# Turning the attention weights of an encoder layer by VectorE blocks and a trip through DRAM instead of by TensorE

## The chip, the cores and the metric

The kernel runs on one core of one Trainium2 chip. The core has five engines with instruction streams of their own: TensorE (PE: matmuls; its weight loads are listed as PEld), VectorE (DVE), ScalarE (ACT), GpSimd (POOL) and SyncE (SP). Each works through its stream in order and waits on semaphores. SP here does nothing but issue DMAs, POOL mostly issues DMAs; the transfers run on 16 DMA engines that all queues share. The metric is the device time of one execution in microseconds.

## What is computed

One encoder layer over 1024 positions of width 1024, in float32: a SwiGLU block, a mixer, and a second SwiGLU block, each followed by a layer norm. The change lies in the mixer's attention:

```python
HEAD_DIM = 128
ATTN_PATTERNS = ((128, 1), (512, 4), (2048, 16))     # (window, dilation), 4 heads each
# Query i attends to i + dilation*j for |j| <= window/(2*dilation), i.e. 64 keys to each side
s = einsum(q, k) * scale + bias(masked)
p = exp(s - max(s))
den = sum(p)
o = einsum(p, v) / den
# the three groups' outputs are then mixed by softmax over their log-sum-exps
attn = sum(softmax(lse over groups) * o)
```

With the scores computed as queries (partitions) by keys (columns), the exponentials p have to be turned to keys by queries before they can be multiplied with v.

## The kernel before

Large products are computed by a Strassen-like scheme: a block of output channels is seven products (`PROD`, jobs `J[c, 1]` to `J[c, 7]`), each job twelve matmuls of 128x128 by 512 columns (each operand split in a high and a low part, three terms). The mixer's projection runs over pairs of channel blocks: two for the Fourier branch, then twelve that give the queries and keys of one head each, then eight for the gates. The twelve heads go in four slots `h`, in each of them group `g` 0, 1, 2 (dilation 1, 4, 16). The attention of a head is done while the projections of later pairs run: its small matmuls are put between the jobs.

A head's attention goes in steps (`one(si, step)`); a step holds two query tiles (four in group 2):

| group | steps per head | query tiles x keys of a step |
|---|---|---|
| 0 | 4 | three of 2 x 256, one of 2 x 192 (the first and last tile) |
| 1 | 4 | 2 x 192 |
| 2 | 2 | 4 x 128 |

That makes 40 steps. A step of width 192 is called split in the code (`split_`). Each step is a chain over the engines:

1. `scores`: TensorE, into a PSUM bank `sc`.
2. `add_bias`: VectorE, from PSUM to a half page `p` in SBUF (scale and bias; the 256-wide form keeps 192 of the keys of each tile, packed as 384 columns).
3. `top`: VectorE, row maxima. `exps`: ScalarE, exponentials in place, with row sums.
4. `turn`: TensorE, transposes of 128x128 blocks (`cuts`: three for the widths 256 and 192, two for group 2) into a PSUM bank `pt`.
5. `blank`: VectorE, zeros into the parts of the turned tile `pT` that are masked (not for split steps). `turned`: ScalarE, the copy of `pt` into `pT`.
6. `values`: TensorE, three or four matmuls with the values `v` (and `ve`, the values at the windows' edges), into a PSUM bank `pv`.
7. `keep`: ScalarE, the copy into the head's output page `pv`, which POOL stores to DRAM (`pv_d`). A later part (`combine`) loads these pages again (`pw`) and mixes the groups.

The values are loaded by `load_values` (SP, from `v_spill`, in rows of 512 bytes, two to seven DMAs a head), the bias by `load_bias` (POOL), the weights of the next projections by `pair_load` (SP: `gq`, `uq`, 512 KB each).

The order on every engine is fixed when the program is built, by a planner written into the kernel (`Flow`). It has one node for each piece of work, with a booked cost, the nodes it depends on, and the buffers that it takes and gives back: 8 PSUM banks (`b`), 46 pages of 4 KB per partition (`p`) and 14 half pages (`h`). `fl.job` nodes make up TensorE's main sequence, in a given order. `V`, `S` and `G` nodes are work of VectorE, ScalarE and POOL, taken by urgency when the planner's clock of that engine comes to them. `F` nodes are floating TensorE work, such as the steps' matmuls: at each job boundary those are put in whose inputs were ready 0.8 us before. `Q` nodes are loads issued on SP: at each job boundary those are issued whose time has come and whose inputs exist. They are booked on one clock of the DMA engines:

```python
    RATE, LAND, STORE, KEEP = 0.36, 2.5, 3.5, 4
...
            self.dma = max(self.dma, t) + n.cost / self.RATE
            self.finish(n, self.dma + self.LAND)
```

The cost is in MB, the rate in MB per us. POOL's stores are booked on the same clock. In a dependency written `(node, w)` the planner adds `w` us behind the node. The booked figures decide the order only; on the chip every instruction waits for its real inputs, in the order of its engine. A DMA that reads what another has written waits on SP until that one has landed.

Of the kernel before, what the change touches and what calls it, by code (L numbers as in the profile page):

```python
# [16 lines left out]
P = 128  # L17
# [26 lines left out]
PAIRS = 11  # L44
FIRST = 3
MIDK = 36
LEADS = [0, 1, 2, 3, (0, 1), (1, 1), (2, 1), (3, 0), (4, 0), (5, 0), (3, 1), (4, 1), (5, 1)]


# [29 lines left out]
class Flow:  # L79
# [207 lines left out]
class Builder:  # L287
# [10 lines left out]
    def half(self, name, dt=F32):  # L298
        return self.sb.tile([P, 512], dt, name=name, tag="s2", bufs=NS2)
# [4 lines left out]
    def bank(self, name):  # L304
        return self.pp.tile([P, 512], F32, name=name, tag="ps", bufs=8)
# [6 lines left out]
def kernel(  # L312
# [40 lines left out]
    W, B, H, J = {}, {}, {}, {}  # L353
# [998 lines left out]
    for i, (to, x0, x1) in enumerate((("t1", "b11", "b12"), ("t3", "b12", "b22"), ("t2", "t1", "b22"),  # L1352
# [16 lines left out]
    for i, (to, x0, x1) in enumerate((("t1", "b11", "b12"), ("t3", "b12", "b22"), ("t2", "t1", "b22"),  # L1369
# [11 lines left out]
        n = Q(J[("a", 5 + i), 4], 0.6, copy, [ttn[x0]] if x0 in ttn else [], lead=0.0)  # L1381
# [109 lines left out]
    qt = V(0.4, third_row, [q2], VJ["t", 6, 0], halves=1)  # L1491
# [255 lines left out]
    last_turn = [None, None]  # L1747

    def attention(idx, g, h, qk, qk_nodes):
        c = PC["q", idx]  # L1750
        env = {}
        qv = Q(J[c, 4], 0.5, lambda: env.__setitem__("v", load_values(g, h)),
               [(n, 4.0) for m in range(8) for n in (v_stored[g, m] if g == 2 else [v_stored[g, m]])], 12.0, pages=1 + int(g == 0),
               halves=int(g == 1))
        qb = Q(J[c, 4], 0.1, lambda: env.__setitem__("b", load_bias(g, h)),
               [(shear_n[g * SLOTS + h], 4.0)] + ([bias_done[idx - 2]] if idx >= 2 else []), 12.0)
# [10 lines left out]
        if g == 0:  # L1767
            qk_nodes = [split(f"{'qk'[i]}s{h}", lambda i=i: qk[i], lambda t, i=i: qk_parts.__setitem__(i, t), qk_nodes[i])
                        for i in range(2)]
        else:  # L1770
            qk_nodes = qk_nodes[0] + qk_nodes[1]
        exp_n.setdefault(h, [])

        def one(si, step):
            n, w = len(step), step[0][2]
            pw = 64 if w == P else 192
            st = {}
# [34 lines left out]
            tiles = sorted(qt for qt, _, _ in step)  # L1812
# [12 lines left out]
                                         accum_out=stats[h][:, k, 1:2])  # L1825
            (qa, ka, _), (qb_, kb_, _) = step[0], step[1]
            cuts = [0, P] if w == P else [0, 2 * P, P]
            where = [(qa, ka), (qb_, kb_ + 64)] if w == 192 else [(qa, qa * P), (qb_, qb_ * P)] if w == 256 else []

            def turn():  # L1830
                st["tp"] = ps = bank(f"pt{g}{h}{si}")
                flat = st.pop("p")
                for sl, x in enumerate(cuts):
                    nc.tensor.transpose(ps[:, sl * P:(sl + 1) * P], flat[:, x:x + P], ident)

            split_ = w == 192
# [5 lines left out]
                nc.vector.memset(t[64:P, :, 0:64], 0.0)  # L1842

            def turned():
                if split_:
                    st["t"] = half(f"pT{g}{h}{si}")
                t, tp = st["t"], st["tp"]
                k = 0
                if w > P:
                    k = 2 * P  # L1850
                    nc.scalar.activation(t[:, :k], tp[:, :k], AF.Copy)
                if split_:
                    to, at = (x[:, k:k + P].rearrange("p (s q) -> p s q", s=2) for x in (t, tp))
                    nc.scalar.activation(to, at[:, ::-1, :], AF.Copy)
                    return
                to = t[:, k:].rearrange("p (n q) -> p n q", q=P)
                at = tp[:, k:k + (512 - k) // 2].rearrange("p (n q) -> p n q", q=64)
                for ps_ in (slice(0, 64), slice(64, P)):
                    nc.scalar.activation(to[ps_, :, ps_], at[ps_], AF.Copy)

            def values():
                st["o"] = bk = bank(f"pv{g}{h}{si}")
                by_half = bk.rearrange("p (r a) -> p r a", a=64)
                pt = st.pop("t")

                def add(out, v, sl, start, stop):
                    nc.tensor.matmul(out, v, pt[:, sl * P:(sl + 1) * P], start=start, stop=stop, skip_group_check=True)  # L1867
                if w == P:
                    for i in range(4):
                        r = 4 * (i // 2) + i % 2  # L1870
                        add(by_half[:, r:r + 3:2, :], env["v"][tiles[0] + i], i, True, True)
                    return
                for i, (qt, k0) in enumerate(where):
                    at = tiles.index(qt) * P
                    add(bk[:, at:at + P], env["v"][k0, P], i, i == 0, False)
                if split_:
                    add(bk[:, 64:192], env["v"]["edge", ka], 2, False, True)
                else:
                    for i in range(2):
                        add(by_half[:, i:i + 3:2, :], env["v"]["edge", qa, i], 2 + i, False, True)  # L1880

            def keep():
                if "pv" not in env:
                    env["pv"] = page(f"pv{g}{h}")
                pv, bk = env["pv"], st.pop("o")
                q0, q1 = tiles[0], tiles[1]
                if split_:
                    dst = (pv.rearrange("p (t q) -> p t q", q=P)[:, 0:8:7, :] if g == 0 else
                           pv.rearrange("p (a r) -> p r a", r=4)[:, q0 // 2, :])
                    src = bk[:, 0:2 * P].rearrange("p (t q) -> p t q", q=P) if g == 0 else bk[:, 0:2 * P]  # L1890
# [7 lines left out]
            f1 = F((0.224, 0.324, 0.36)[(w - P) // 64] * n, scores, qk_nodes + [x for x in (last_turn[0], qv, qb) if x], 1,  # L1898
                   gives=(4 if g == 0 else 2) if end else 0)
            n1 = V((0.75, 0.55, 0.75)[g if not split_ else 1], add_bias, [f1], frees=1, halves=1, slack=8.0)  # L1900
            if end:
# [7 lines left out]
            f3 = F(0.22 * (3 if split_ else 4), values, [n4], 1, hgives=1 + int(end and g == 1), gives=1 + int(g == 0) if end else 0)  # L1909
# [103 lines left out]
    for i, (to, x0, x1) in enumerate((("t1", "b11", "b12"), ("t3", "b12", "b22"), ("t2", "t1", "b22"),  # L2013
# [6 lines left out]
        n = Q(SUMS0AT[i][0], 1.15, copy, [wtn[x0]] if x0 in wtn else [], lead=0.0)  # L2020
# [68 lines left out]
    at = [VJ[p, m] for p in (5, 4, 3) for m in range(4)] + [J[PC[c], p] for c in pairs[:11] for p in PROD]  # L2089
# [95 lines left out]
    for gi in range(4):  # L2185
        st = {}
# [4 lines left out]
        q = Q(PJ[0], 0.5, load, [(uf_n[gi], 4.0)], 14.0 - gi, pages=1)  # L2191
        t_, s_ = divmod(gi, 2)
        for i in range(2):
# [24 lines left out]
            f = F(0.88, run, [q, (chan_ready, 10.0)], 1, gives=i)  # L2218
            n = S(0.42, hi, [f], pages=1 if s_ == 0 else 0, slack=2.0)
# [43 lines left out]
    for t in range(2):  # L2263
        st = {}
# [172 lines left out]
    for c in range(8):  # L2437
        c2, cc = divmod(c, 2)
        st = {}
# [329 lines left out]
```

## Time and profile before

| | |
|---|---|
| median of three runs | 2026.43 us (2026.42 to 2026.71) |
| span of the profiled execution, first to last instruction | 2024.4 us |
| between the span and the median | 2.0 us |
| TensorE busy | 2018.2 us, 100% of the span |
| VectorE, ScalarE, POOL busy | 1385.4, 910.3, 283.9 us |
| attention steps | 815 to 1105 us of the span |
| mean rate of the DMA engines | 228 GB/s over the span |

How to read the rows. A line such as `L1834 PE MATMUL pt<-ident,p 128*128 128x128 f32 x3` names the line of the kernel, the engine, the operation, the output and the inputs by tile name, the shape, and how many instructions it stands for. In a timeline the first two columns are start and duration in us; a matmul's duration reaches over the start of the next, since they are pipelined, so what one costs is read from the distance of starts. In rows of groups the figures behind the bar are busy time in us and the mean of one in ns, then the idle time of the engine just before, with what ended it. `SPq` is the issue of a DMA by SP; "to landing" is counted from the issue's start until the data has arrived. A line of waits has the total in us, how often, and the longest. In a DMA queue's row stand its packets, the MB moved and the share of the time of all 16 engines.

### The profile page before, as it was taken

How to read it: one execution, taken by the hardware profiler on the slowest of the kernel's cores; microseconds unless marked ns; L12 is line 12 of the kernel's file. 1: busy time of each engine (PE TensorE's matmuls, PEld its weight loads, DVE VectorE, ACT ScalarE, POOL GpSimd, SP SyncE). 2: the span in 40 equal slices, each digit the busy share in tenths (PEclk: the TensorE clock that was granted, in tenths of full speed). 3: DMA queues.
4: the chain of work that ended last, by engine and by line, in shares of the span. 5: the costliest groups of instructions: out<-in, count | busy, mean ns of one | idle time of the engine just before them, and what ended most of it. 6: DMA issues, size and time to landing. Idle time of an engine off the chain costs nothing.

```text
span 2024.4 us, 26430 instructions
## 1 busy us (share of the span) xinstructions
PE 2018.2 (100%) x9525; PEld 1693.1 (84%) x9525; DVE 1385.4 (68%) x2040; ACT 910.3 (45%) x1465; POOL 283.9 (14%) x484
## 2 busy tenths in 40 slices
PE   9999999999999999999999999999999999999998
PEld 8888888888888898888888888888888888888887
DVE  7765665576676878665666766887877666575566
ACT  7332433454464224665556444336533333355342
POOL 0233211111001132222122110000011111110000
PEclk9999999999999999999999999999999999999999
DMA  5789998899853386665355669883257877668753
GB/s 208 250 260 281 316 301 242 250 344 390 313 188 136 97 293 221 218 176 163 123 153 178 208 237 340 319 325 147 79 187 244 262 247 220 176 216 289 238 184 97
DMA packets 185795, 461.42 MB, mean 228 GB/s; under 512 B 21886, under 2 KB 62414, under 8 KB 185120
## 3 DMA queue, kind: packets, MB, share of 16 engines
q1 hardware_dynamic: 137376, 302.31, 43.1%
q0 software_dynamic: 48288, 157.42, 25.9%
q8 instruction: 75, 1.23, 0.2%
q14 instruction: 56, 0.46, 0.1%
HBM read 344.59 MB, written 185.29 MB: 262 GB/s over the span
## 4 chain that ended last, share of the span: by engine, by line
PE 100%; DVE 0%; DVEq 0%; issue 0%
PE Ab L502 14%; PE Aa L502 14%; PE Aq L502 8%; PE Db L502 6%; PE Da L502 6%; PE As L502 5%; PE Dq L502 3%; PE Xb L934 3%; PE Zb L934 3%; PE Za L934 3%; PE Xa L934 3%; PE Ds L502 2%; PE wA L2519 2%; PE pv L1867 2%; PE Va L934 1%; PE Vb L934 1%
## 5 line engine op out<-in xcount | busy, mean ns | idle before, releaser
L344 POOL DMA_DIRECT2D n_spill<-y x16 | 9.4, 586 | 304.5 <-DVE y L1134 233.7
L1824 ACT ACTIVATE p<-p,stat 128x192 f32<-128x192 f32 (+1 forms) x96 | 39.2, 409 | 28.1 <-DVE stat L1819 28.0
L344 POOL DMA_DIRECT2D hsba<-t2b x21 | 11.6, 552 | 265.2 <-DVE t2b L793 265.2
L344 POOL DMA_DIRECT2D hsaa<-t2a x21 | 12.9, 613 | 232.3 <-DVE t2a L793 227.1
L696 ACT ACTIVATE t2b<-Ab 128x512 f32<-128x512 f32 x21 | 12.6, 600 | 63.5 <-PE Ab L502 63.5
L789 DVE TENSOR_TENSOR t2b<-Db,t2b 128x512 f32<-128x512 f32 x21 | 14.5, 691 | 38.7 <-PE Db L502 38.7
L1119 ACT ACTIVATE y<-ya,ls 128x1024 f32<-128x1024 f32 x16 | 18.4, 1150 | 47.4 <-DVE ls L1114 36.8
L696 ACT ACTIVATE t2a<-Aa 128x512 f32<-128x512 f32 x21 | 12.6, 599 | 60.3 <-PE Aa L502 60.3
L789 DVE TENSOR_TENSOR t2a<-Da,t2a 128x512 f32<-128x512 f32 x21 | 14.5, 689 | 34.0 <-PE Da L502 34.0
L781 DVE TENSOR_TENSOR t3b<-Db,t3b 128x512 f32<-128x512 f32 x21 | 14.5, 691 | 22.5 <-PE Db L502 21.0
L502 PE MATMUL Da<-Xs40h,usa 128*128 128x512 f32 x84 | 29.3, 389 | 0.0
L502 PE MATMUL Da<-Xs41h,usa 128*128 128x512 f32 x84 | 29.3, 389 | 0.0
L502 PE MATMUL Db<-Zs40h,usb 128*128 128x512 f32 x84 | 29.3, 389 | 0.0
L502 PE MATMUL Db<-Zs41h,usb 128*128 128x512 f32 x84 | 29.3, 389 | 0.0
L781 DVE TENSOR_TENSOR t3a<-Da,t3a 128x512 f32<-128x512 f32 x21 | 14.5, 691 | 21.4 <-PE Da L502 20.6
L2609 POOL TENSOR_SCALAR zd<-ident,ls 128x128 f32<-128x128 f32 x1 | 0.4, 375 | 202.0 <-DVE ls L2618 202.0
L1589 DVE SCALAR_TENSOR_TENSOR oq<-Dq,b_cols,t3q 128x512 f32<-128x512 f32 x12 | 11.9, 989 | 24.5 <-PE Dq L502 24.4
L1867 PEld LDWEIGHTS pv<-pT,v 128*128 128x128 f32 x192 | 25.9, 191 | 1.7
L1867 PE MATMUL pv<-pT,v 128*128 128x128 f32 x192 | 27.2, 274 | 0.0
L696 ACT ACTIVATE t3b<-Ab 128x512 f32<-128x512 f32 x21 | 12.6, 601 | 26.0 <-PE Ab L502 25.8
L344 POOL DMA_DIRECT2D y_spill<-n x16 | 8.8, 551 | 96.1 <-DVE n L1150 96.1
L696 ACT ACTIVATE t3a<-Aa 128x512 f32<-128x512 f32 x21 | 12.5, 596 | 21.7 <-PE Aa L502 21.6
(7704 smaller groups left out, 7537.4 us busy)
## 6 DMA issues: line engine op xcount, KB each, us to landing
qa<-hsas SPq DMA_DIRECT2D x43, 256.0 KB, 5.2
qa<-tdat SPq DMA_DIRECT2D x43, 256.0 KB, 5.2
qb<-hsbs SPq DMA_DIRECT2D x43, 256.0 KB, 3.8
ga<-in_ffn_gu_dram SPq DMA_DIRECT2D x21, 512.0 KB, 8.4
ua<-in_ffn_gu_dram SPq DMA_DIRECT2D x21, 512.0 KB, 9.3
gb<-in_ffn_gu_dram SPq DMA_DIRECT2D x21, 512.0 KB, 4.5
ub<-in_ffn_gu_dram SPq DMA_DIRECT2D x21, 512.0 KB, 6.5
qb<-tdbt SPq DMA_DIRECT2D x33, 256.0 KB, 4.2
```

The costliest lines, as they stand in the source:

```text
L344: nc.gpsimd.dma_start(*a, **kw)
L502: nc.tensor.matmul(out, pick(w, a)[:, k * P:(k + 1) * P], self.cols(xn, b, k), start=first and k == 0 and ti == 0, stop=last and k == kt - ...
L696: nc.scalar.activation(H[c, t], B[c, "B"], AF.Copy)
L781: nc.vector.tensor_sub(H[c, "t3"], B[c, "D"], H[c, "t3"])
L789: nc.vector.tensor_sub(H[c, "t2"], B.pop((c, "D")), H[c, "t2"])
L934: nc.tensor.matmul(bank_, a, b, start=first and ti == 0, stop=last and ti == len(todo) - 1, skip_group_check=True)
L1119: nc.scalar.activation(st["y"], st["a"], AF.Square, bias=s[:, 2:3], scale=1.0, accum_out=s[:, 3:4])
L1589: stt(views(pages_[i], hf), views(b, None), bias[i], views(H.pop((c, t)), None), op0=OP.add, op1=op)
L1824: nc.scalar.activation(p3()[:, i, :], p3()[:, i, :], AF.Exp, bias=stats[h][:, k, 0:1], scale=1.0, accum_out=stats[h][:, k, 1:2])
L1867: nc.tensor.matmul(out, v, pt[:, sl * P:(sl + 1) * P], start=start, stop=stop, skip_group_check=True)
L2519: nc.tensor.matmul(B["w", bk, m], X4.cols(xn, a, k)[:, m * P:(m + 1) * P], pick(w, b), start=new and k == 0 and ti == 0, stop=k == 3 and t ...
L2609: nc.gpsimd.tensor_scalar(st["d"], ident, s()[:, 0:1], -1.0 / D, op0=OP.mult, op1=OP.mult)
```

## The change

`FAR_STEPS = (4, 2, 0)` gives, by group, how many of a head's steps are turned in a new way: all four of group 0, the first two of group 1, none of group 2; with four heads a group, 24 of the 40 steps. In such a far step

- `turn` is one VectorE transpose of 128x384, which turns each 32x32 block in place of its own (a new half page `px`, for split steps the later `pT` itself);
- `away` (SP) stores the result to a DRAM tile `pd` so that the blocks come to lie in turned order, in four DMAs, one for each 32 partitions, each with 32 x 12 runs of 32 elements (128 bytes);
- `blank` follows the transpose, not the maxima;
- `turned` (SP) loads the tile `pT` from `pd`: one DMA with 3 rows of 512 bytes for each partition in a split step, otherwise one with 2 rows of 512 bytes and two with 64 partitions x 2 rows of 256 bytes;
- `values` is as before, but in split steps the turned tile has its queries in another order, so its matmuls write PSUM in halves of 64 columns with a stride, and `keep` reads them in that order.

The other 16 steps go on as before (`pe_turn`, `pe_turned`). Two dependencies move for all steps: the load of the values is awaited by `values` and no longer by `scores`; and `scores` of a step waits for the turning, in whichever way, of the second step before it, as it did.

```diff
+FAR_STEPS = (4, 2, 0)
...
+            far = si < FAR_STEPS[g]
...
             def turn():
+                st["t" if split_ else "x"] = x = half(f"px{g}{h}{si}")
+                nc.vector.transpose(x[:, :384], st.pop("p")[:, :384])
+
+            def away():
+                st["d"] = d = kb.dram([3, P, P], f"pd{g}{h}{si}")
+                x = st["t"] if split_ else st.pop("x")
+                for a in range(4):
+                    nc.sync.dma_start(bass.AP(tensor=d.tensor, offset=d.offset + 32 * a, ap=[[P, 32], [32 * P, 12], [1, 32]]),
+                                      x[32 * a:32 * a + 32, :384].rearrange("p (m c) -> p m c", c=32))
+
+            def pe_turn():
                 st["tp"] = ps = bank(f"pt{g}{h}{si}")
...
             def turned():
+                t, d = st["t"], st.pop("d")
+
+                def rows(dst, slot, row, n_, step_, w_):
+                    src = bass.AP(tensor=d.tensor, offset=d.offset + (slot * P + row) * P, ap=[[P, dst.shape[0]], [step_, n_], [1, w_]])
+                    nc.sync.dma_start(dst, src)
+                if split_:
+                    rows(t[:, :3 * P].rearrange("p (n q) -> p n q", q=P), 0, 0, 3, P * P, P)
+                    return
+                rows(t[:, :2 * P].rearrange("p (n q) -> p n q", q=P), 0, 0, 2, 2 * P * P, P)
+                for b in range(2):
+                    to = t[64 * b:64 * b + 64, 2 * P:].rearrange("p (n q) -> p n q", q=P)[:, :, 64 * b:64 * b + 64]
+                    rows(to, 1, 64 * b, 2, 64, 64)
+
+            def pe_turned():
...
-            f1 = F(..., scores, qk_nodes + [x for x in (last_turn[0], qv, qb) if x], 1,
+            f1 = F(..., scores, qk_nodes + [x for x in (last_turn[0], qb) if x], 1,
...
-            f2 = F(0.11 * len(cuts), turn, [n3], 1, hgives=1)
-            nb = [] if split_ else [V(0.54 if w == P else 0.35, blank, [n2], slack=8.0, halves=1)]
-            n4 = S(0.6 if split_ else 0.76 if w == P else 0.9, turned, [f2] + nb, frees=1, halves=0 if nb else 1, slack=8.0)
-            f3 = F(0.22 * (3 if split_ else 4), values, [n4], 1, ...)
+            if far:
+                nt = V(0.5, turn, [n3], halves=1, hgives=1, slack=8.0)
+                at = J[c, 7]
+                q2 = Q(at, 0.18, away, [nt], 60.0, hgives=0 if split_ else 1)
+                nb = [] if split_ else [V(0.35, blank, [nt], slack=8.0, halves=1)]
+                q4 = Q(at, 0.18, turned, [(q2, 1.0)] + nb, 60.0)
+            else:
+                nt = F(0.11 * len(cuts), pe_turn, [n3], 1, hgives=1)
+                nb = [] if split_ else [V(0.54 if w == P else 0.35, blank, [n2], slack=8.0, halves=1)]
+                q4 = S(0.6 if split_ else 0.76 if w == P else 0.9, pe_turned, [nt] + nb, frees=1, halves=0 if nb else 1, slack=8.0)
+            f3 = F(0.22 * (3 if split_ else 4), values, [q4, qv], 1, ...)
...
-            last_turn[:] = [last_turn[1], f2]
+            last_turn[:] = [last_turn[1], nt]
```

More of the change, by code (lines that the diff above doesn't have):

```diff
@@ L1873, in values @@
                 for i, (qt, k0) in enumerate(where):
-                    at = tiles.index(qt) * P
-                    add(bk[:, at:at + P], env["v"][k0, P], i, i == 0, False)
+                    at = tiles.index(qt)
+                    if split_ and far:
+                        add(by_half[:, at:at + 3:2, :], env["v"][k0, P], 2 * i, i == 0, False)
+                    else:
+                        add(bk[:, at * P:at * P + P], env["v"][k0, P], i, i == 0, False)
                 if split_:
-                    add(bk[:, 64:192], env["v"]["edge", ka], 2, False, True)
+                    add(bk[:, 64:192], env["v"]["edge", ka], 1 if far else 2, False, True)
                 else:
@@ L1897, in one @@
             end = si == len(steps) - 1
-            f1 = F((0.224, 0.324, 0.36)[(w - P) // 64] * n, scores, qk_nodes + [x for x in (last_turn[0], qv, qb) if x], 1,
+            f1 = F((0.224, 0.324, 0.36)[(w - P) // 64] * n, scores, qk_nodes + [x for x in (last_turn[0], qb) if x], 1,
                    gives=(4 if g == 0 else 2) if end else 0)
@@ L1905, in one @@
             exp_n[h].append(n3)
-            f2 = F(0.11 * len(cuts), turn, [n3], 1, hgives=1)
-            nb = [] if split_ else [V(0.54 if w == P else 0.35, blank, [n2], slack=8.0, halves=1)]
-            n4 = S(0.6 if split_ else 0.76 if w == P else 0.9, turned, [f2] + nb, frees=1, halves=0 if nb else 1, slack=8.0)
-            f3 = F(0.22 * (3 if split_ else 4), values, [n4], 1, hgives=1 + int(end and g == 1), gives=1 + int(g == 0) if end else 0)
+            if far:
[4 more added lines that the diff above has]
+                q4 = Q(at, 0.18, turned, [(q2, 1.0)] + nb, 60.0)
+            else:
+                nt = F(0.11 * len(cuts), pe_turn, [n3], 1, hgives=1)
+                nb = [] if split_ else [V(0.54 if w == P else 0.35, blank, [n2], slack=8.0, halves=1)]
+                q4 = S(0.6 if split_ else 0.76 if w == P else 0.9, pe_turned, [nt] + nb, frees=1, halves=0 if nb else 1, slack=8.0)
+            f3 = F(0.22 * (3 if split_ else 4), values, [q4, qv], 1, hgives=1 + int(end and g == 1), gives=1 + int(g == 0) if end else 0)
             n5 = S(0.45 if w > P else 1.0, keep, [f3], frees=1, pages=0 if si else 1, slack=8.0)
             done_values.append(n5)
-            last_turn[:] = [last_turn[1], f2]
+            last_turn[:] = [last_turn[1], nt]
         for si, step in enumerate(steps):
```

5 lines of the change are left out of this document (3 added, 2 removed).

## The prediction

> **What bounds the kernel now.** I read the page first, then the waits of TensorE, then the attention stage by windows, then TensorE's timeline around a transpose.
>
> ```profile
> span 2024.4 us, 26430 instructions
> ...
> PE 2018.2 (100%) x9525; PEld 1693.1 (84%) x9525; DVE 1385.4 (68%) x2040; ACT 910.3 (45%) x1465; POOL 283.9 (14%) x484
> ...
> q1 hardware_dynamic: 137376, 302.31, 43.1%
> ```
>
> ```profile
> PE zr L2612 <- POOL zd L2609: 1.4, 1, 1.4
> PE warm L2668 <- DVE one L331: 0.9, 1, 0.9
> ```
>
> ```profile
> core 0: us, PE busy (x) PEld busy (x) DVE busy (x) ACT busy (x) POOL busy (x), PEclk, DMA share, GB/s
> 815.00:1105.00 290.00, 290.00 (x1573) 250.54 (x1572) 190.58 (x334) 179.93 (x451) 54.12 (x93) 1.00 0.54 166
> ```
>
> The second fence is the whole list of TensorE's waits: one at the start, one at the end, none between. The third is the stage that the change touches: all 40 attention steps lie between 815 and 1105 us, TensorE is busy 290.00 of 290 us at a granted clock of 1.00, VectorE 66%, the DMA engines 54%. So the kernel's time is the sum of TensorE's issue steps. A matmul taken away shortens it by its step, and any wait put into TensorE's stream lengthens it in full, since nothing there is idle to absorb it.
>
> The profiled execution's span is 2024.4 us, the median of the runs 2026.43. I carry the 2.0 us between them unchanged.
>
> **What the change removes.** Group 0 has all its four steps turned the new way, group 1 two of its four, group 2 none: 6 steps in each of 4 head slots, 24. Each drops three TensorE transposes. TensorE's timeline around two such places (start, duration):
>
> ```profile
> 852.14 0.49 PE L1834 MATMUL pt<-ident,p 128*128 128x128 f32 x3
> 852.38 0.48 PE L502 MATMUL Aq<-Ya110h,gq5h 128*128 128x512 f32 x1
> 852.70 0.39 PE L502 MATMUL Aq<-Ya110l,gq5h 128*128 128x512 f32 x1
> 852.93 0.39 PE L502 MATMUL Aq<-Ya110h,gq5l 128*128 128x512 f32 x1
> ...
> 895.18 0.81 PE L1834 MATMUL pt<-ident,p 128*128 128x128 f32 x6
> 895.76 0.48 PE L502 MATMUL Aq<-Ya220h,t34q6h 128*128 128x512 f32 x1
> 896.07 0.40 PE L502 MATMUL Aq<-Ya220l,t34q6h 128*128 128x512 f32 x1
> ```
>
> Durations overlap, so I go by starts. One 512-column matmul costs 0.23 us (852.93 - 852.70). From the first transpose to the second matmul behind it is 852.70 - 852.14 = 0.56 us, of which one matmul's 0.23 stays: three transposes cost 0.33 us. Two steps together cost 896.07 - 895.18 - 0.23 = 0.66, the same per step. The gain on TensorE is 24 x 0.33 = **8.0 us**, or 0.39%; it cannot be more, because the values matmuls keep their number and size (only the order of columns in PSUM changes).
>
> ScalarE loses the evictions behind those transposes, and VectorE gains a transpose:
>
> ```profile
> L1819 DVE TENSOR_REDUCE stat<-p 128x2 f32<-128x384 f32 x32 | 16.6, 549 | 0.5
> L1851 ACT ACTIVATE pT<-pt 128x256 f32<-128x256 f32 x32 | 12.4, 387 | 8.0 <-PE pt L1834 7.9
> L1859 ACT ACTIVATE pT<-pt 64x128 f32<-64x128 f32 x24 | 6.4, 266 | 0.1
> L1854 ACT ACTIVATE pT<-pt 128x128 f32<-128x128 f32 x20 | 5.8, 288 | 0.0
> ```
>
> ScalarE: 24 of the 387 ns, all 24 of the 266 ns, 12 of the 288 ns, 19 us less, off the path. VectorE: 24 transposes of 128x384. No row shows one; the nearest is the reduction of the same 128x384 at 549 ns, and the other bound is twice that if four-byte elements pass twice. I take 0.55: 13 us more on an engine with 99 us free in the stage. The memsets were there before. On the path it is only a link of the chain below, where the planner books it at 0.5. The Trainium skill (VectorE: DVE Perf Modes, The three transpose paths) gives 311 ns for 128x128 in two-byte elements, in 32x32 blocks; three of these, an estimate of 0.93 us, would lengthen each chain by 0.4 us and leave the sum as it is.
>
> **What it adds: a round trip on SP's queue.** Each far step puts four stores on SP, each waiting for the VectorE transpose, and then the reload (one DMA in a split step, three in a 256-wide one), which waits until the stores have landed. In all 96 stores and 48 reloads. SP runs in order, so behind those waits stand the weight, value and combine loads.
>
> ```profile
> 830.63 2.59 SPq L1712 DMA_DIRECT2D v<-v_spill  x4
> ...
> 876.08 0.33 SPq L632 DMA_DIRECT2D gq<-in_in_pairs_dram  x1
> ...
> 901.80 0.33 SPq L632 DMA_DIRECT2D gq<-in_in_pairs_dram  x1
> 902.23 2.66 SPq L1712 DMA_DIRECT2D v<-v_spill  x4
> ```
>
> ```profile
> L1712 SPq DMA_DIRECT2D ve<-v_spill x24: 476/608/1525, 859.2 to 1035.2; - x24
> ...
> DMA to landing us min/median/max: 2.4/4.0/6.6
> ```
>
> ```profile
> L2581 SPq DMA_DIRECT2D out_dram<-z x7: 332/338/344, 1966.9 to 2014.8; - x7
> L2637 SPq DMA_DIRECT2D out_dram<-z x3: 332/384/399, 2020.9 to 2021.8; - x3
> ...
> DMA to landing us min/median/max: 1.8/2.6/2.7
> ```
>
> Four issues of many short rows take 2.6 us, 0.65 each. A load of 512-byte rows lands 2.4 to 6.6 us after its issue (median 4.0), a store from SP after 1.8 to 2.7 (2.6). At the medians a 256-wide step needs 3 x 0.65 + 2.6 until the stores are there, then 2 x 0.65 + 4.0 until the last reload is: 9.85 us; a split step 1.95 + 2.6 + 4.0 = 8.55. SP itself is held 6.5 us (1.95 + 2.6 + 1.95) or 5.2 us.
>
> What sets where TensorE meets this is the order fixed at build time by the kernel's planner. It books 0.18/0.36 + 2.5 = 3.0 us for the stores, 1.0 between, 3.0 for the reload: 7.0 us in all and 4.5 us between steps, and puts the values matmul into the stream at the first job boundary at least 0.8 us later. These figures order the program; they are no durations. A job is twelve matmuls, 12 x 0.23 = 2.7 us. The planner issues the stores at a job boundary, 1.4 us after the transpose on average, while SP starts as soon as the transpose is done; the values fall on a boundary again, another 1.4. So a lone step has 0.8 to 6.2 us in hand, on average 3.6, against a shortfall of 9.85 - 7.0 = 2.85 (or 1.55). It fits on average, with two or three jobs as cover; if that cover is gone, each step costs TensorE the shortfall.
>
> Group 0's four steps queue on SP. If they come without a gap, each takes 6.5 us where 4.5 are booked: the second is 2.85 + 2.0 - 3.6 = 1.25 us late, the third 3.25, the fourth, a split one, 1.55 + 6.0 - 3.6 = 3.95. Waits at the earlier steps count in the later ones, so the ceiling at these medians is about 4 us per group-0 head, 16 in all. Group 1's two split steps stay in hand (1.55 + 0.7 - 3.6 < 0). The floor is zero, for two reasons: the planner books all other transfers, also POOL's stores, on the same clock at 360 GB/s, and the stage moves 166 GB/s, 46% of it, which adds up to 2 us to each 4.5 booked while in the trace POOL's stores hold SP not at all; and the steps come in pairs, not as four. I take 0.5 us per head, near the floor: **2.0 us** given back.
>
> The weight loads behind the round trip have this in hand:
>
> ```profile
> gq<-in_in_pairs_dram SPq DMA_DIRECT2D x9, 512.0 KB, 5.0
> ```
>
> ```profile
> L364 ACT ACTIVATE gq7h<-gq x1: 1054/1054/1054, 881.3 to 881.3; 128x1024 fp32r<-128x1024 f32 x1
> ...
> L364 ACT ACTIVATE gq8h<-gq x1: 1047/1047/1047, 912.7 to 912.7; 128x1024 fp32r<-128x1024 f32 x1
> ```
>
> The load issued at 901.80 lands after 5.0 at 906.8 and is first read at 912.7: 5.9 us. The one issued at 876.08 lands at 881.1 and is read at 881.3: 0.2 us, but it is issued behind group 2, which puts nothing new on SP. One service of 6.5 us, 4.5 of it booked, does not use up 5.9. I cost these at nothing; bounds are zero and, where ScalarE does stand still for one head's load, the 2 us not booked, 4 x 2 = 8 us. The same loads would be next to be late.
>
> Data: 96 packets of 128 bytes per DMA engine and step. No row has such packets.
>
> ```profile
> q1 hardware_dynamic: 2144, 1.19, 52.5%
> ```
>
> That is 934 to 942 us, nearly all 512-byte rows: 0.525 x 16 x 8 us / 2144 = 31 ns for 555 bytes. Over the run (first fence) it is 0.431 x 16 x 2024 / 137376 = 102 ns for 2,200. The line through both gives 13 ns at 128 bytes; the upper end among rows is the 31 ns. So 1.2 to 3.0 us per step, mostly under the 2.6 us in which the four stores are issued. Over 24 steps that is 30 to 72 us of time on all engines, where 46% of 290 us, 133 us, is free.
>
> Sum: 2026.4 - 8.0 + 2.0 = **2020.4 us**.
>
> **Rivals.** *Gain given back* (2026.4): weights late by the bound above, or half the queue's ceiling, 8 us. For it: the loads' spread of 2.4 to 6.6. Against: the planner's own reserve.
>
> *Slower by SP's queue* (2034): the services come without a gap and the booking of other traffic does not help; TensorE waits at group 0's values for 16 us, 2026.4 - 8.0 + 16. It decides from 2 us of waiting per group-0 head, which four 256-wide and split services in a row reach at 6.0 and 4.7 us (0.5 below the medians). For it: my own 6.5. Against: no TensorE wait in the present program, although a head's four values loads, 1.95 + 4.0 us, land 2 us after the 3.9 (0.5/0.36 + 2.5) that the planner books.
>
> *Short writes cost double.* If a 128-byte write is a read and a write, it costs 2 x 31 ns, the engines need 96 x 62 ns = 6.0 us per step, 3.4 us more than the issues cover, and a service takes 9.9 us. With 2 us of other bookings each step slips 3.4 further than booked: the fourth of group 0 by 12 us, group 1's second by 3.5, so 15 x 4 = 60 us: 2078. No row bears on it either way; the Trainium skill speaks for it (DMA: Bandwidth & Descriptors, Specifications): transfers below 512 B are done as read-modify-write. No trace here shows that.
>
> That the transposes cost nothing now is excluded by the 0.56 us above.
>
> **How the numbers follow.** Forecast 0.50; given back 0.18; slower by the queue 0.21; short writes 0.11. A measurement of this kernel can tell 0.2%, 4.1 us, so the first is faster, the second the same, the others slower. The range starts at the full gain, 2018, and goes to 2041 to take in the queue case up to services of 6.9 us (0.43 above the medians: 3.95 + 4 x 0.43 = 5.7 us per head); the short writes are left out. The forecast's own range is 2018 to 2022.3.
>
> **What would show it.** In the new profile TensorE has 40 transposes, not 112, and the stage is 6 to 8 us shorter. Right: TensorE's waits on pv for the reloaded pT stay under 3 us in sum, stores to pd land within about 3 us of their issue, SP is held about 6 us per step. Wrong: waits before group 0's values matmuls that grow from the first step to the fourth (queue), landings of pd above 5 us (short writes), or ScalarE and VectorE standing idle until gq or uq land (weights).

## The result, and the profile after

The changed kernel takes 2032.61 us, the median of seven runs (2029.12 to 2035.1), against 2026.59 for the kernel before in the same batch (2026.42 to 2026.79): 1.003 times the time, 95% interval 1.0021 to 1.004. It is slower by 0.3%, where 0.3% faster was forecast. The runs of the changed kernel lie 6 us apart, those of the kernel before 0.4: what is lost varies from run to run. The profiled run took 2034.63 us, near the upper end, and its span is 8.5 us longer than before's.

From the page after, the span and the engines' busy time:

```profile
span 2032.9 us, 26474 instructions
...
PE 2015.0 (99%) x9453; PEld 1687.1 (83%) x9453; DVE 1395.5 (69%) x2064; ACT 893.0 (44%) x1405; POOL 282.9 (14%) x484
```

9525 - 9453 = 72 matmuls are gone, 3 for each of the 24 far steps. TensorE is busy 3.2 us less in a span that is 8.5 us longer, so it now stands still. Its waits (us in total, times, longest us):

```profile
PE pv L1894 <- DMA px<-pd: 5.3, 2, 3.7
PE pv L1894 <- ACT pT L1886: 3.1, 2, 2.2
PE pv L1894 <- DMA pT<-pd: 2.5, 1, 2.5
```

Left out are `zr` and `warm`, there before with the same 1.4 and 0.9 us, and 0.7 us in two waits at `pt` for ScalarE. New are 7.8 us before values matmuls whose turned tile (`pT`, or `px` in a split step) is still on its way back from DRAM, and 3.8 us before work of group 2, which ScalarE has not delivered. The three waits for reloads lie at the fourth step of group 0 in slot 0 (3.7 us), the third in slot 1 (2.5) and the second step of group 1 in slot 3 (1.6). The longest wait, in TensorE's timeline:

```profile
852.25 0.68 PE L1894 MATMUL pv<-px,v 128*128 128x128 f32 x4 [3.68 <-DMA px<-pd]
...
853.95 0.77 PE L503 MATMUL Aq<-Ya110h,gq5h 128*128 128x512 f32 x1
...
856.63 0.39 PE L503 MATMUL Aq<-Ya111h,gq5h 128*128 128x512 f32 x1
```

SP's timeline for that head's four trips (L1840 are the stores, L1862 the reloads, start and duration of the issues):

```profile
821.98 1.90 SPq L1840 DMA_DIRECT2D pd<-px  x4
825.37 1.60 SPq L1862 DMA_DIRECT2D pT<-pd  x3
827.07 2.08 SPq L1840 DMA_DIRECT2D pd<-px  x4
831.31 1.60 SPq L1862 DMA_DIRECT2D pT<-pd  x3
...
833.59 0.43 SPq L633 DMA_DIRECT2D gq<-in_in_pairs_dram  x1
834.07 0.43 SPq L633 DMA_DIRECT2D uq<-in_in_pairs_dram  x1
834.54 2.87 SPq L1840 DMA_DIRECT2D pd<-px  x4
843.98 1.89 SPq L1862 DMA_DIRECT2D pT<-pd  x3
845.97 2.08 SPq L1840 DMA_DIRECT2D pd<-px  x4
849.48 0.38 SPq L1862 DMA_DIRECT2D px<-pd  x1
```

The trips follow one another: between them SP issues only three loads, before the third, in 1.5 us. The first holds SP from 821.98 to 826.97, 5.0 us; the third, whose stores go out together with two 512 KB weight loads, from 834.54 to 845.87, 11.3 us. The fourth cannot start before 845.97, its reload goes out at 849.48, and TensorE, which works through its own order, goes on at 852.25. How long the stores of the first and of the third trip took to land, in the DMA issues of the stretches 821.5 to 825 and 834.4 to 838 us (KB each, median us to landing):

```profile
pd<-px SPq DMA_DIRECT2D x4, 48.0 KB, 2.2
```

```profile
uq<-in_in_pairs_dram SPq DMA_DIRECT2D x1, 512.0 KB, 7.4
...
pd<-px SPq DMA_DIRECT2D x4, 48.0 KB, 7.7
```

2.2 us alone, 7.7 us beside the weights (and three 256 KB stores of POOL, left out here). The same thing from the other side: SP's longest wait in sum and two of ScalarE's waits for weights, 805 to 1130 us:

```profile
SPq L1862 <- DMA pd<-px: 58.7, 43, 6.2
```

```profile
ACT gs15h L365 <- DMA gs<-in_in_pairs_dram: 5.8, 1, 5.8
...
ACT gq8h L365 <- DMA gq<-in_in_pairs_dram: 4.9, 1, 4.9
```

SP stands still for 58.7 us with a reload in hand, 43 times, and weight loads behind it are late: these two, and gq9h in the same way by 4.5 us. In the kernel before ScalarE has no such wait in this stage.

### The profile page after: what moved, and what is told of

Read it like the earlier page. It is cut to its first block, busy times and chain, and to the rows that moved or that the text cites. A ratio compares the mean times of both kernels' runs of the same rounds, so it can differ in the third digit from the quotient of the medians.

```text
span 2032.9 us, 26474 instructions
## 1 busy us (share of the span) xinstructions
PE 2015.0 (99%) x9453; PEld 1687.1 (83%) x9453; DVE 1395.5 (69%) x2064; ACT 893.0 (44%) x1405; POOL 282.9 (14%) x484
## 4 chain that ended last, share of the span: by engine, by line
PE 92%; DMA 3%; issue 2%; DVE 1%; SPq 1%; ACT 0%; POOL 0%; DVEq 0%; ACTq 0%; POOLq 0%
PE Ab L503 14%; PE Aa L503 14%; PE Db L503 6%; PE Da L503 6%; PE Aq L503 5%; PE As L503 5%; PE Zb L935 3%; PE Xb L935 3%; PE Za L935 3%; PE Xa L935 3%; PE Dq L503 2%; PE Ds L503 2%; PE wA L2557 2%; PE Va L935 1%; PE Vb L935 1%
## 5 line engine op out<-in xcount | busy, mean ns | idle before, releaser
L345 POOL DMA_DIRECT2D hsba<-t2b x21 | 11.6, 550 | 265.7 <-DVE t2b L794 265.7
L697 ACT ACTIVATE t2b<-Ab 128x512 f32<-128x512 f32 x21 | 12.6, 600 | 63.8 <-PE Ab L503 63.8
L697 ACT ACTIVATE t2a<-Aa 128x512 f32<-128x512 f32 x21 | 12.6, 600 | 61.5 <-PE Aa L503 61.5
L1590 DVE SCALAR_TENSOR_TENSOR oq<-Dq,b_cols,t2q 128x512 f32<-128x512 f32 x12 | 11.9, 991 | 20.9 <-PE Dq L503 20.8
L1894 PEld LDWEIGHTS pv<-pT,v 128*128 128x128 f32 x144 | 19.2, 191 | 8.1 <-ACT pT L1886 3.9
L1894 PE MATMUL pv<-pT,v 128*128 128x128 f32 x144 | 20.2, 276 | 5.5 <-ACT pT L1886 3.1
L697 ACT ACTIVATE t3b<-Ab 128x512 f32<-128x512 f32 x21 | 12.6, 600 | 26.1 <-PE Ab L503 25.8
```

The costliest lines, as they stand in the source:

```text
L345: nc.gpsimd.dma_start(*a, **kw)
L697: nc.scalar.activation(H[c, t], B[c, "B"], AF.Copy)
L1590: stt(views(pages_[i], hf), views(b, None), bias[i], views(H.pop((c, t)), None), op0=OP.add, op1=op)
```

## The experiments

Each was timed in a batch with the kernel before, which took 2026.57 to 2026.58 in the first two batches and 2026.39 in the last; the changed kernel itself was timed in the batch of the result.

| run | what differs from the changed kernel | us | ratio to before, 95% |
|---|---|---|---|
| e1_no_trip | values read VectorE's output, no DMA | 2019.35 | 0.9964, 0.995 to 0.9978 |
| e2_stores_only | stores, no reload | 2020.45 | 0.9971, 0.9959 to 0.9982 |
| e3_pool | trip issued by POOL | 2054.62 | 1.0139, 1.0122 to 1.0155 |
| e4_strict | reload later in SP's order | 2021.79 | 0.9977, 0.9967 to 0.9986 |
| e5_book | more time booked per trip | 2025.66 | 0.9996, 0.9986 to 1.0005 |
| e6_strict_440 | e4 with 32 far steps | 2023.6 | 0.9986, 0.9976 to 0.9995 |
| e8_g0_only | group 0 only, 16 steps | 2027.26 | 1.0004, 0.9994 to 1.0013 |
| e9_pairs | two steps each of groups 0 and 1 | 2022.62 | 0.9981, 0.9972 to 0.9991 |
| e7_no_far | no far step | 2026.58 | 1.0001, 0.9991 to 1.001 |
| e11_w_pool | weights issued by POOL | 2034.39 | 1.004, 1.0026 to 1.0054 |
| e4b_strict2 | e4, stores later in SP's order too | 2020.7 | 0.9973, 0.9964 to 0.9983 |
| e10_strict_220 | e4 with e9's steps | 2021.93 | 0.9979, 0.997 to 0.9988 |

**Is the gain there? e1_no_trip and e2_stores_only.** In both the values matmuls take VectorE's output directly, which is turned only within blocks of 32x32, so the attention's result is another one; reloads and zeros are left out in both, the stores only in e1.

```diff
-                q2 = Q(at, 0.18, away, ...)
-                nb = ...
-                q4 = Q(at, 0.18, turned, [(q2, 1.0)] + nb, 60.0)
+                q4 = nt                     # e2 keeps q2, and lets nobody wait for it
```

> Leaves out the trip through DRAM: in the 24 far steps the values matmuls read the VectorE transpose's output directly (blocks not in turned order, no blanking), so no stores, no reloads, no waits on them. Theory queue (the 14 us lost stand entirely in the waits that the trip causes on SP's queue and the DMA rings behind it): the full gain of 8.0 us, 2018.6 us, no TensorE wait in the attention stage. Rival order (the VectorE transposes and the moved dependencies re-order the stage and cost by themselves): above 2022 us, with TensorE waits left on ScalarE or VectorE.

> As the kernel without the trip, but the 96 stores to pd are issued on SP; no reload, and nothing waits for the stores to land. Theory queue: SP stands still only for the VectorE transposes, the weight loads behind are delayed by 2 to 3 us at most, no values matmul waits: 2018.6 to 2020.5 us. Rival short writes (the 128-byte writes themselves load the 16 DMA engines): above 2024 us, gq and uq landing more than 2 us later than before and ScalarE waiting for them.

e1: 2019.35, 7.2 us under before; the whole gain of 8.0 would be 2018.6. e2: 2020.45. Of TensorE's waits on the far steps are left, first in e1, then in e2:

```profile
PE pv L1894 <- DVE px L1834: 0.4, 2, 0.2
```

```profile
PE pv L1894 <- DVE px L1834: 2.1, 3, 1.8
```

So fewer transposes bring what they should, VectorE's transpose is in time but for one wait of 1.8 us in e2, and 96 stores of 128-byte pieces cost about 1 us. The 12.2 us between e2 and the changed kernel come with the reload, the zeros ahead of it, and what waits for it.

**Is it SP's order? e4_strict.** The planner puts a DMA into SP's order as soon as its inputs have a place in the order, even if they are booked to land later; `strict` holds it back until the planner's clock has reached the booked landing. The loads of weights and values, and the stores of the next step, come ahead of it.

```diff
-                q4 = Q(at, 0.18, turned, [(q2, 1.0)] + nb, 60.0)
+                q4 = Q(at, 0.18, turned, [(q2, 1.0)] + nb, 60.0, strict=True)
```

> The reload is put into SP's order only at the job boundary at which the planner expects the stores to have landed, not directly behind them; the next step's stores and the weight loads go in between. Theory queue: SP's 58.7 us of waits on pd shrink below 15 us, the weight loads are issued on time; values are planned up to one job later: 2019 to 2024 us. Rival (SP's waits are harmless, the trip's own latency against the booked 7 us is what counts): 2031 to 2035 us.

2021.79, 10.8 us less than the changed kernel, with the same DMAs. The same stretch of SP's timeline, the stores among the DMA issues of 831 to 839 us, TensorE's one wait for a reload, and SP's for the stores to land:

```profile
822.21 4.08 SPq L1840 DMA_DIRECT2D pd<-px  x8
...
826.98 3.45 SPq L1862 DMA_DIRECT2D pT<-pd  x6
830.47 0.59 SPq L633 DMA_DIRECT2D gq<-in_in_pairs_dram  x1
831.10 0.46 SPq L633 DMA_DIRECT2D uq<-in_in_pairs_dram  x1
831.67 6.94 SPq L1840 DMA_DIRECT2D pd<-px  x8
838.72 3.18 SPq L1713 DMA_DIRECT2D v<-v_spill  x4
841.99 1.75 SPq L1862 DMA_DIRECT2D pT<-pd  x3
843.84 0.54 SPq L1862 DMA_DIRECT2D px<-pd  x1
```

```profile
pd<-px SPq DMA_DIRECT2D x8, 48.0 KB, 5.4
```

```profile
PE pv L1894 <- DMA pT<-pd: 0.8, 1, 0.8
```

```profile
SPq L1862 <- DMA pd<-px: 3.5, 5, 1.3
```

SP stands still before reloads for 3.5 us instead of 58.7. Two trips now overlap, and other loads fill the time in which stores land. The stores beside the weights still take 5.4 us, but nobody stands behind them: the last reload of this head is issued at 843.84 instead of 849.48. The edit also shifts the order on the other engines, since everything is placed by the same clock, so it is not SP's order alone that differs; and the profiled run took 2020.14 us, the fastest of ten, so its waits are rather few.

**Or is too little time booked? e5_book.** SP's order is built by the same rule as in the changed kernel; more time is booked between stores and reload and behind the reload, as the diff has it.

```diff
-                q4 = Q(at, 0.18, turned, [(q2, 1.0)] + nb, 60.0)
+                q4 = Q(at, 0.18, turned, [(q2, 3.0)] + nb, 60.0)
...
-            f3 = F(..., values, [q4, qv], 1, ...)
+            f3 = F(..., values, [(q4, 3.0 if far else 0.0), qv], 1, ...)
```

> SP's order rule stays (the reload directly behind its stores), but the planner books 4 us more for a trip: 2 more between stores and reload, so the reload and the loads behind it are planned later, and 2 more until the values. Theory queue with late values as its larger part (7.8 of the 12.7 us of TensorE waits in the changed kernel were on the reload, and 1.9 us of slow clock behind them): the values waits go, the weight loads still stand behind SP's waits and cost TensorE 2 to 5 us: 2020 to 2025 us. Rival head of line (SP standing still for the landing is what matters, however late the values are planned): above 2028 us.

2025.66: 7 us better than the changed kernel, but no better than the kernel before. Two of TensorE's waits, and SP's for landings:

```profile
PE fc L2235 <- issue: 1.5, 1, 1.5
...
PE pv L1894 <- ACT pT L1886: 0.8, 1, 0.8
```

```profile
SPq L1862 <- DMA pd<-px: 53.1, 46, 3.6
```

TensorE no longer waits for a reload, but SP still stands still for 53.1 us. The time lies between the two expected ranges, and the waits for weights, which were to cost 2 to 5 us, do not show. TensorE's waits beside `zr` and `warm` are 4.3 us in sum, 3.5 of them after the attention stage; why the other 3 us of the 8.0 are missing stays open. So late values seem to be part of the loss, but e4's order wins 3.9 us more.

**How many trips in a row? e8_g0_only and e9_pairs.** Both have 16 far steps, 5.3 us of gain: four in a row in each head of group 0, or two in a row in groups 0 and 1.

```diff
-FAR_STEPS = (4, 2, 0)
+FAR_STEPS = (4, 0, 0)        # e8_g0_only;   e9_pairs: (2, 2, 0)
```

> The changed kernel with group 0's four steps a head only (16 far steps). Full gain 16 x 0.33 = 5.3 us. Theory queue (four trips in a row behind one another and behind the weight loads): the waits stay at group 0's last steps and at the weight loads, 6 to 12 us: 2027 to 2033 us. Rival (it is the six trips a slot, with group 1's two behind group 0's four, that overfill SP): waits under 3 us, 2021 to 2024 us.

> The changed kernel with the first two steps of group 0 and of group 1 (also 16 far steps, in pairs with a pause between). Full gain 5.3 us. Theory queue: a pair's second trip is at most one service late and the pause empties SP: waits under 3 us, 2021 to 2024 us. Rival (a cost per trip, by bandwidth or by the weight loads that happen to stand behind one): as with group 0 alone, 2026 to 2033 us.

e8: 2027.26; e9: 2022.62, of which 2026.57 - 5.3 = 2021.3 would be all. TensorE's waits for a reload in e8:

```profile
PE pv L1894 <- DMA pT<-pd: 2.3, 2, 2.0
```

With 0.5 us in a split step it is 2.8. In e9 there are none. The same number of steps is worth 4 us if the trips come in pairs and nothing if they come in fours. A price per trip does not fit: both have 64 stores, and e9 has 32 reload DMAs against 40 in e8, but loses 1.3 us of the 5.3 and e8 6.0. The two differ in which steps are turned, too. e8 is 6.0 us above the 2021.3, and the waits name only 3.3 of them (0.5 for ScalarE); where the others went stays open.

**Another queue? e3_pool.** POOL issues the trip instead of SP, in the same program order of TensorE, VectorE and ScalarE.

```diff
-                    nc.sync.dma_start(dst, src)
+                    nc.gpsimd.dma_start(dst, src)       # and the stores the same way
```

> The whole trip, but its 96 stores and 48 reloads are issued by POOL in place of SP, at the same places of the planner's order. Theory queue: gq and uq are issued on time again and the stores no longer stand behind two weight loads in SP's rings, so the ScalarE waits on gq go and the values waits shrink to under 5 us; but POOL's own stores (wot, pv_d, cb) now stand behind the waits: 2019 to 2027 us. Rival short writes or bandwidth (which queue issues them does not matter): 2031 to 2035 us, the values waits as before.

2054.62, the slowest of all, and outside both expected ranges. POOL's issues of the stores (ns min/median/max), the trip that meets the weights, and TensorE's waits:

```profile
L1840 POOL DMA_DIRECT2D pd<-px x96: 616/626/679, 822.8 to 1107.7; - x96
```

```profile
829.73 2.46 POOL L1840 DMA_DIRECT2D pd<-px  x4
836.68 1.91 POOL L1862 DMA_DIRECT2D pT<-pd  x3 [4.49 <-DMA pd<-px]
```

```profile
PE pv L1894 <- DMA px<-pd: 15.2, 9, 3.4
PE pv L1894 <- DMA pT<-pd: 7.1, 7, 2.0
```

ScalarE's waits for gq shrink to 0.2 us, since the weights no longer stand behind a trip. But the queue has only moved: POOL stands still before the reload, a store's issue costs 0.63 us instead of 0.48, and the 22.3 us before the values are three times the changed kernel's 7.8. Weights that come in time do not save the trip.

**The weights' place, or their data? e11_w_pool.** Now the weights move to POOL and the trip stays on SP, again with the other engines' orders unchanged.

```diff
-            nc.sync.dma_start(t, w[c[1], i])
+            (nc.gpsimd if c[0] == "q" else nc.sync).dma_start(t, w[c[1], i])
```

> The changed kernel, with the 24 weight loads of the mixer's projection (gq and uq, 512 KB each) issued by POOL instead of SP; the order on TensorE, VectorE and ScalarE is the same, instruction by instruction. Theory (stores that stand directly behind two weight loads on SP's queue land 7 to 8 us late, and weights issued behind a trip are late): no store to pd lands later than about 4 us, the group-0 trips take about the undisturbed 6.5 us, TensorE's waits on pv for a reloaded pT fall under 2 us and its waits on ACT before group 2's values go too, if POOL issues the weights in time; 2019.5 to 2023. Rival (it is SP's waiting in order, four trips in a row, and the weights only happen to stand between them): the waits on pv for the reloads keep at least half of their 7.8 us, 2025 to 2030. Second rival (two 512 KB loads take the DMA engines from any other transfer, whichever queue issues them): stores to pd still land at 7 to 8 us, waits as before, 2029 to 2034.

2034.39, as slow as the changed kernel: my theory of that moment, that the stores land late because they stand behind the weights in the same queue, falls. TensorE's waits for reloads are not under 2 us but 9.7, though in a profiled run of 2040.61 us, the slowest of five:

```profile
PE pv L1894 <- DMA pT<-pd: 5.6, 2, 3.8
PE pv L1894 <- DMA px<-pd: 4.1, 4, 2.5
```

POOL issues the first of two weight loads (the second 0.5 us later), and SP at that time the second trip; the window holds it:

```profile
826.55 0.54 POOL L633 DMA_DIRECT2D gq<-in_in_pairs_dram  x1 [7.47 <-PE sc L1789]
```

```profile
826.55 2.20 SPq L1840 DMA_DIRECT2D pd<-px  x4
832.97 1.60 SPq L1862 DMA_DIRECT2D pT<-pd  x3
```

```profile
826.50:833.00 6.50, 6.50 (x34) 5.54 (x33) 5.55 (x11) 3.74 (x12) 2.71 (x5) 1.00 0.85 249
```

The trip that meets the weights holds SP 8.0 us (826.55 to 834.57) though they come from another queue; in that window the DMA engines are 0.85 busy (the last column but one). The transfers share the engines, whoever issues them. The Trainium skill says so too (DMA: Bandwidth & Descriptors, Issuing engines are not separate DMA queues); here it is 4.7 us for stores beside POOL's weights, 7.7 beside SP's own and 2.2 alone. The 4.7 and the 7.7 are not the same trip in the same company (one 256 KB store of POOL against three), and other stores of this run take up to 8.8 us, so how much the shared queue adds stays open. What stands of the theory is the trips in a row; the weights matter at least by their data.

**The moved dependency: e7_no_far.** No far step; only the later wait for the values is left of the change (`FAR_STEPS = (0, 0, 0)`).

> The changed program with no far step at all (steps by group 0, 0, 0): all 40 steps are turned on TensorE. What is left of the change is that the values are awaited by the values matmuls and no longer by the scores. Theory (the moved dependency costs and gives nothing): 2026.6, within 0.2% of the kernel before, no wait on TensorE. Rival (the moved dependency itself lets the values come late, and part of the loss is due to it): waits of TensorE at pv on v or ve, 2028 or more.

2026.58, and no TensorE wait beside `zr` and `warm`: it costs nothing.

**Versions that beat both: e4b_strict2, e10_strict_220, e6_strict_440.** e4b makes the stores `strict` too, e10 joins e4 with e9, e6 has e4's order with all four steps of group 1 (`(4, 4, 0)`).

> As the run in which the reload waits in the planner's order for the stores, and the stores too are put in SP's order only when VectorE's transpose is expected to be done; 24 far steps. Theory (what is left of SP's standing still, 41 us at the stores for the transpose, keeps weights late): those waits fall under 15 us and the time to between 2019 and 2021.5. Rival (SP's waits at the stores are harmless, and a later issue makes the trips end later): 2021.5 to 2025, with waits at pv.

> The reload put in SP's order only at the place where the planner expects the stores to have landed, together with two far steps per head in groups 0 and 1 and none in group 2 (16 of 40 steps). Gain on TensorE at most 16 x 0.33 = 5.3 us. Theory (trips in pairs and an SP that does not stand waiting cost nothing): 2021.3 to 2022, the floor of the gain. Rival (some weight loads still land late and ScalarE behind them): 2023 or more, with waits of TensorE on ACT.

> The late reload of the run before (reload put into SP's order only when its stores are expected to have landed), and now all eight steps of groups 0 and 1 turned the new way, 32 of 40. Eight more steps take 8 x 0.33 = 2.7 us more from TensorE. If SP has room once it no longer waits for landings: 2021.8 - 2.7 = 2019.1 us. Rival (the eight more trips, 32 stores and 8 reloads, fill SP or the DMA rings again): 2022 us or more, values waits in group 1.

e4b: 2020.7 (2019.44 to 2024.56), the fastest of the complete programs, 0.27% under the kernel before; that it beats e4 (2020.14 to 2023.26) the runs do not show. Its TensorE waits 0.2 us for a reload, yet SP waits 32.8 us at the stores for VectorE, so the expectation's under 15 was wrong, and those waits did little harm: the time fell into the expected range all the same. e10: 2021.93, 4.5 of its 5.3 us. e6: 2023.6, with eight more steps, 2.6 us more to gain, is slower than e4 by 1.8:

```profile
PE pt L1847 <- ACT p L1825: 3.4, 2, 3.2
```

The wait of 3.2 us ends at 871.72 us. Read back through ScalarE and VectorE, it begins with a load of another kind (`wot31r`) that SP issues behind the stores of two trips:

```profile
859.70 0.63 ACT L2102 ACTIVATE wot31h<-wot31r 128x512 fp32r<-128x512 f32 x1 [4.61 <-DMA wot31r<-wtt]
```

```profile
868.00 0.69 DVE L2106 TENSOR_TENSOR wot21l<-wot21r,wot21h 128x512 fp32r<-128x512 f32 x1 [4.86 <-DMA wot_d<-wot31h]
```

VectorE stands until POOL's store of `wot31h` has landed, and the step's scale, maxima and exponentials come behind. Then from 870 to 880 us the granted clock is 0.66, and twelve 512-column matmuls take 0.43 us each instead of 0.23, about 2.4 us more. So the price of the next trips is again a load that comes late behind them, as the trace reads; no run takes this chain apart.

## Why the prediction was wrong, point by point

- **The gain of 8.0 us: right.** The distances between matmul starts in the two traces give about 8 us for the 72 transposes, and e1, with nothing in the way, gets 7.2 of it.
- **VectorE's transpose at 0.55 us: right.** Its 24 took 531 to 581 ns. The 0.93 us that I had worked out from the Trainium skill (VectorE: DVE Perf Modes, The three transpose paths) is too high for this shape.

```profile
L1834 DVE STREAM_TRANSPOSE px<-p x24: 531/570/581, 821.4 to 1069.4; 128x384 f32<-128x384 f32 x24
```

- **Short writes: rightly left out.** Stores to pd land after 1.6 us at best and 2.7 in the median (8.1 at worst, beside the weights). Between 822 and 825 us, where SP moves almost only these, 1606 packets took 42.3% of 16 engines' 3 us, 12.6 ns each, where the line through two rows had given 13. A read and a write at 62 ns, which the rule of the Trainium skill (DMA: Bandwidth & Descriptors, Specifications) had suggested as a rival, does not show. The sign that I had named for it, landings above 5 us, did come, but the 7.7 us stand beside weights and POOL's stores; the sign could not tell this rival from company.

```profile
q1 hardware_dynamic: 1606, 0.21, 42.3%
```

- **The trip at 9.85 us: too long alone, too short in company.** Alone the first trip takes about 6.5 us to the last landing, SP held 5.0 (I had 6.5): an issue costs 0.48 us instead of 0.65, stores land in 2.2 and reloads in 2.1 instead of 2.6 and 4.0. Beside weights and POOL's stores it holds SP 11.3. The four trips of this head held it 5.0, 5.8, 11.3 and 3.9 us: the medians (2.7 us for stores, near my 2.6, and 2.3 for reloads) hide the one that counts.
- **The queue of group 0: the step that failed.** I had put the ceiling at 4 us a head, and then taken 0.5, "near the floor", because the planner books other traffic on the same clock and because the steps come in pairs. Neither holds in the changed kernel. The planner puts a reload into SP's order as soon as its stores and zeros have their places, whatever landing it has booked, so what it books leaves no room in SP's order. The steps did come in pairs before (slot 1: six transposes each at 895.18 and 907.23 us), but now the trips of that head start at 898.79, 904.07, 910.48 and 916.07, each right behind the last, with two weight loads inside the third. And the traffic of this stretch is not the stage's mean of 54%: from 835 to 840 us the engines were 0.81 busy at 273 GB/s. The term was 2.0 us; the waits for reloads came to 7.8, of which 1.6 at group 1, whose steps I had taken to stay in hand.
- **The rival *slower by SP's queue* (0.21, 2034 us): right in kind, its time in part by luck.** The queue is what happened, and slot 0 waits at the fourth step. But the rival's 16 us of waiting, 4 in each head, from services of one length are not there: two heads of group 0 wait, 3.7 and 2.5 us, where one trip went beside weight loads. The rest of the loss came from ScalarE and the clock, which were not in its sum.
- **The weight loads at nothing: wrong.** I had set 5.9 us in hand for gq8 against 2 us not booked. It was issued at 912.61 us instead of 901.80, and ScalarE waited 4.9 us for exactly that load. No TensorE wait for ScalarE follows that one directly. There are 0.9 us at 954.40, 12 us behind ScalarE's wait for gq9h, and 2.9 us from 1101 to 1107, behind its wait for gs15h, a load of the gates that I had not looked at; ahead of the last 2.2 of these it waits for a store of `pv_d`, too. In sum they are 3.8 us, inside the bound of 8. That the late weights cause them is read from the order of the waits; no run isolates it.
- **Not in the sum at all: the clock.** After the wait of 3.7 us the next six 512-column matmuls take 2.68 us (853.95 to 856.63), 0.45 each instead of 0.23, and the window 850 to 860 shows a granted clock of 0.83:

```profile
850.00:860.00 10.00, 7.75 (x39) 6.88 (x40) 2.40 (x3) 4.77 (x11) 2.15 (x4) 0.83 0.79 226
```

  That is 1.3 us over 6 x 0.23; with the transposes and values ahead of them some 1.8. The Trainium skill (TensorE: Matmul & The Clock Gate, What's actually happening) says that a window of about 3.4 us without work brings the clock to half; the step of 0.45 agrees with it. The length of a wait alone did not decide it here: behind the wait of 2.5 us the window 918 to 928 shows 1.00, and in e3_pool the clock stays at 1.00 around a wait of 3.3 us (1110 to 1120) and is 0.83 behind one of 2.0 (1084 to 1094).

Together: -8.0 for the transposes, +11.6 in the listed new waits, +1.8 for the clock, 5.4 of the 8.5 us between the spans. Distances of matmul starts that grew beyond 0.6 us add some 12.7, a little more than the list; the remaining 2 us lie in many small distances, which I cannot put down to one cause. That the range held the time is due to the queue case, not to the forecast.

## What to carry to other kernels

A load that waits for another DMA's landing blocks everything behind it on its issuing queue (SP stood 58.7 us that way here). Price such a trip by how long it holds the queue, at the traffic of the very stretch where it falls, and ask what is issued behind it; a mean over the stage says little. If several trips come in a row, issue the stores of the next ones and other loads ahead of the reload: the same DMAs then cost 2 to 3 us of the 8.0 gained instead of 14 (2020.7 and 2021.8 against 2032.6 us here).

## What the runs showed that I had not expected

- A short wait of TensorE can cost more than its length: 3.7 us of standing still were followed by 2.7 us of 512-column matmuls at half the rate, in e6 3.2 us by over 5 us of them.
- Moving weight loads to another issuing engine did not make the stores beside them fast: 4.7 us against 2.2 alone, at a DMA share of 0.85.
- The trip on POOL was 22 us slower than on SP. Its 96 stores took 0.63 us to issue instead of 0.48 and its 48 reloads 0.60 to 0.76 instead of 0.38 to 0.52, about 22 us more of issuing over the 290 of the stage; that the two figures agree proves nothing, since issuing is not all on TensorE's path. What else makes POOL's trips long was not taken apart.
- Stores of 128-byte pieces were cheap: 48 KB in 1.6 to 2.5 us where nothing else ran.
